# The second rows of the merge's operand in single steps, two latencies of the planned order, and the last block's sum ahead of its product

## The chip, the cores and the metric

The kernel runs on one core of a Trainium2 chip. A core has five engines that run their own instruction streams and wait for each other on semaphores: TensorE (PE, with weight loads as PEld) for matmuls, VectorE (DVE), ScalarE (ACT), GpSimd (POOL) and SyncE (SP), which issues nearly all DMAs, in the order of its stream. The metric is the device time of one execution in microseconds (us).

## The reference

One inference step of a one-layer encoder over 1024 prompt frames and 32 frames of a running stream, all in float32. After a norm and one wide input projection, two branches run side by side, gated linear attention (4 heads) and differential attention (8 heads); then they are merged:

```python
def out_merge(x, o_gla, o_diff, gg, dg, ma, mb, ...):
    yg = rmsnorm(o_gla, gla_norm_g).reshape(B, T, GLA_VAL) * silu(gg)
    yd = (rmsnorm(o_diff, diff_subln_g) * (1.0 - lambda_init)).reshape(B, T, DIFF_VAL) * silu(dg)
    merged = sigmoid(ma) * (yg @ w_proj_gla) + sigmoid(mb) * (yd @ w_proj_diff)
    return x + rmsnorm(merged @ w_out, post_norm_g)
```

Linear attention walks the frames in chunks: with the running sum `b` of the log decays, a chunk's keys are scaled by `exp(b_last - b)` and multiplied with the values into the new state, and each output is a part from the state and a part within the chunk.

## The kernel before

**Projections.** Everything is kept transposed: 128 channels on the partitions, T = 1056 frames (1024 + 32) along the free axis. A float32 operand is split in two, a rounded high part and the remaining low part, and a product is three matmuls (high by high, low by high, high by low). A projection of one block of 128 output channels runs over three chunks of 352 frames, with 8 blocks of the contraction, so 24 matmuls a chunk, into one PSUM bank; an `evac` then takes the bank away. Two banks serve these chunks in turn. Lines L517 to L519 are the matmuls of projections that run as `fill`, L493 to L495 those of the others. Weights come by DMA as `wr`, ScalarE rounds them to `wh` (L483) and GpSimd makes `wl` (L485).

**Stages and order.** Value projections run first, then, from about 216 us, linear attention; from about 543 us differential attention; from about 1137 us the merge's projections, and the output stage behind them. In the attention stages a planner (`Order`, `S.run`) writes TensorE's order: every thread of work yields steps with a cost, the events they need with a latency from the table `W`, and the PSUM banks they take; the planner takes the first thread in the list whose step is ready by its own clock, and projections (`fill`) come last in the list, so that they lie where the other threads wait. In linear attention these threads are a head's chain and the next head's preparation. The latencies are numbers in us; nothing in them changes what is computed. The other engines' instructions are placed by a scheduler that follows this order.

**Names in linear attention.** `k` is scaled by the decay on VectorE (L691), which marks the event `kd`; its transpositions through TensorE go to `ps_kt` (L699), ScalarE rounds them into `kdh` (L701) and VectorE makes `kdl` (L702). `po` is a chunk's output (L766 to L772), `o_sb` its copy in SBUF, scaled by the root mean square (L778); `ps_y` holds its transpositions (L785), `yt` (L788) their product with the gate, stored by DMA. `ps_kt` and `ps_y` take banks of the kind `t`; how long after its matmuls such a bank counts as taken is `kt_t` or `y_t`. `ar` (L619) is the masked part within a chunk; `t` in L573 to L578 is the next head's decay gate.

**The merge.** `w_proj_gla` has eight blocks, pg0 to pg7. Their evacuation, `tha = (1 + tha) * ps` (L1155), is on VectorE; behind a block's third chunk SP stores `tha` (to `ptd`) and loads a later `tha`. The second projection, `w_proj_diff` (L493 to L495), has the operand `yd`, eight rows of 128 channels called `Y` in the trace. Row k is made from the unscaled `ydr` in three steps: `split_yd(k)` multiplies it by `rsb` on VectorE (L1229), rounds it on ScalarE (L1230) into the high half, and subtracts on VectorE (L1231) for the low half; each `rsb` serves two rows and is 1 MB. These rows are made in the completion of pg3 to pg7: pg3 makes row 0, pg4 rows 1 and 2, pg5 row 3, pg6 rows 4 and 5, pg7 rows 6 and 7. In this part VectorE's order is as written. The second projection's evacuation begins with L1250 (`thb`), and the output weights `wout` are split into `cwh` (ScalarE) and `cwl` (VectorE, L1271) beside it.

**The end.** The output stage takes 128 frames at a time; for the last column block ScalarE squares `ps_c` and sums the row (L1300), VectorE multiplies by the weight of the norm (L1301), reduces the sums (L1308, L183), GpSimd takes the power (L184), and VectorE scales the row in two halves (L1317), which are stored. The halves of a block are done when the next block's sum is.

Of the kernel before, what the change touches and what calls it, by code (L numbers as in the profile page):

```python
# [11 lines left out]
F32 = mybir.dt.float32  # L12
# [3 lines left out]
ALU = mybir.AluOpType  # L16
# [9 lines left out]
KT = D // P  # L26
# [3 lines left out]
NQ = NP // P  # L30
# [9 lines left out]
BESIDE = range(3, KT)  # L40
# [14 lines left out]

W = {
# [3 lines left out]
    "tr_t": 2.27, "dv": 5.65, "at": 2.45, "pv_o": 1.6, "sdg": 1.84, "sdk": 21.35, "kc": 7.45, "ss_s": 3.69,  # L60
    "sp": 8.6, "st_t": 1.14, "sv": 3.44, "spt": 0.43, "so_o": 3.58, "so": 4.1, "so_t": 2.9, "yg0": 0.0,
    "yg": 1.18, "pg_b": 1.72, "p": 4.2, "p_w": 0.0042, "s_s0": 1.5, "s_w0": 0.0024, "s_s1": 0.3, "s_w1": 0.0012, "dg": 2.5,
# [68 lines left out]
def hybrid_step_kernel(ctx: ExitStack, tc: tile.TileContext, a):  # L131
# [3 lines left out]
    ve = nc.vector  # L135
    dma = nc.sync.dma_start
    st = nc.sync.dma_start

    def pool(name, bufs=1, **kw):
        return tc.alloc_tile_pool(name=name, bufs=bufs, **kw)  # L140
# [20 lines left out]
    def bank(name):  # L161
        return bank_of("pj", name)
# [18 lines left out]
    def rsqrt_mean(s, w, n, cnt):  # L181

        ve.tensor_scalar(s[0:w, 0:n], s[0:w, 0:n], 1.0 / cnt, EPS, op0=ALU.mult, op1=ALU.add)  # L183
        nc.gpsimd.tensor_tensor(s[0:w, 0:n], s[0:w, 0:n], mhalf[0:w, 0:n], op=ALU.pow)  # L184
# [91 lines left out]
    def sample_tiled(ps, x, w):  # L276

        for k in range(KT):
            r = k % 4 * NS
            mm(ps[r : r + NS], x[:, k, :], w[k], start=k < 4, stop=k >= 4, tile_position=(0, r))  # L280

    def sample_sum(dst, ps):
        act(dst, ps[32:64], AF.Copy)
        for r in (0, 64, 96):
            ve.tensor_tensor(dst, ps[r : r + NS], dst, op=ALU.add)
# [193 lines left out]
    def wtile(b):  # L479
        wr = wp.tile([P, KT, P], F32, tag="wr", bufs=1, name="wr")  # L480
        dma(wr, a["w128"][b])
        wh = odd(wp, KT, P, tag="wh", name="wh")
        act(wh, wr, AF.Copy)  # L483
        wl = odd(wp, KT, P, tag="wl", name="wl")
        nc.gpsimd.tensor_tensor(wl, wr, wh.bitcast(F32), op=ALU.subtract)  # L485
        return wh, wl
# [11 lines left out]
    def fill(jobs, src, then=None):  # L498

        w = wtile(jobs[0][0])  # L500
        for ji, (b, event, begin, needs) in enumerate(jobs):
            wh, wl = w
            evac = done = None
            for t0, n in CHUNKS:
                ps = None
                for k in range(KT):
                    if k % N["fill"] == 0:
                        yield 0.45 * N["fill"], (needs if ps is None else []), (["pj"] if ps is None else [])
                        if evac is None:
                            if ji + 1 < len(jobs):  # L510
                                w = wtile(jobs[ji + 1][0])
                            elif then is not None:
                                ahead.append(wtile(then))
                            evac, done = begin()
                        if ps is None:
                            ps = bank("ps_w")
                    mm(ps[:, :n], wh[:, k, :], src[k][:, 0, t0 : t0 + n], start=(k == 0), stop=False)  # L517
                    mm(ps[:, :n], wl[:, k, :], src[k][:, 0, t0 : t0 + n], start=False, stop=False)  # L518
                    mm(ps[:, :n], wh[:, k, :], src[k][:, 1, t0 : t0 + n], start=False, stop=(k == KT - 1))  # L519
                with tc.high_priority(offset=N["evac"]):  # L520
                    evac(ps[:, :n], slice(t0, t0 + n))
                S.free("pj", W["w_pj"])
            done()
            S.mark(event)

    ahead = []

    def silu_into(dst):

# [618 lines left out]
    def load_tha(j):  # L1148
        if j < KT:
            tha[j] = ld("tha")  # L1150
            dma(tha[j], thd[0, j])

    def pg_evac(j):
        def evac(ps, sl):
            ve.scalar_tensor_tensor(tha[j][:, sl], tha[j][:, sl], 1.0, ps, op0=ALU.add, op1=ALU.mult)  # L1155
        return evac
# [28 lines left out]
    def pg_job(j):  # L1185
        def begin():
            def done():
                st(ptd[j], tha[j])
                load_tha(j + 2)
                if j >= BESIDE[0]:  # L1190
                    for k in range(KT * (j - BESIDE[0]) // len(BESIDE), KT * (j + 1 - BESIDE[0]) // len(BESIDE)):
                        split_yd(k)
            return pg_evac(j), done
        return BLK_PG + j, ("pg", j), begin, []

# [6 lines left out]
    gpost = cp.tile([P, D], F32, name="gpost")  # L1202
    dma(gpost, a["gpost"].to_broadcast([P, D]))
    Y = x_pair("Y")
    yd = [Y[k // 6][:, k % 6] for k in range(KT)]
# [9 lines left out]
    rsb, ydr = {}, {}  # L1215

    def load_yd(k):
        if k < KT:
            ydr[k] = cp.tile([P, T], F32, tag=("cwr", "cwl")[k % 2], name="ydr")
            dma(ydr[k], ydd[k])  # L1220

    def load_rsb(k):
        if k < KT:
            rsb[k // 2] = cp.tile([P, 2, NP], F32, tag="cwh", name="rsb")
            dma(rsb[k // 2], rsd[k : k + 2, :].unsqueeze(0).to_broadcast([P, 2, NP]))

    def split_yd(k):
        r = ydr[k]
        ve.tensor_tensor(r[:, 0:NP], r[:, 0:NP], rsb[k // 2][:, k % 2], op=ALU.mult)  # L1229
        act(yd[k][:, 0, :], r, AF.Copy)  # L1230
        ve.tensor_tensor(yd[k][:, 1, :], r, yd[k][:, 0, :].bitcast(F32), op=ALU.subtract)  # L1231
        if k % 2:
            load_rsb(k + 1)
        load_yd(k + 2)

    load_rsb(0)
    load_yd(0)
# [4 lines left out]
    for j in range(KT):  # L1242
# [6 lines left out]
        def evac(ps, sl, th=th, pt=pt, y=y):  # L1249
            ve.scalar_tensor_tensor(th[:, sl], th[:, sl], 1.0, ps, op0=ALU.add, op1=ALU.mult)  # L1250
            ve.tensor_tensor(pt[:, sl], pt[:, sl], th[:, sl], op=ALU.add)
            act(y[:, 0, sl], pt[:, sl], AF.Copy, scale=0.5)
            ve.scalar_tensor_tensor(y[:, 1, sl], pt[:, sl], 0.5, y[:, 0, sl].bitcast(F32), op0=ALU.mult, op1=ALU.subtract)
# [20 lines left out]
    op = pool("op", reuse_waits="tile")  # L1274
    mgs = sample_whole(mg, op, "mgs")
    oga = xp.tile([P, 4, D], F32, tag="x2", name="oga")
    og = [oga[:, n] for n in range(4)]
# [6 lines left out]
    def out_block(u, n, i, wh, wl, raw):  # L1284
        csl = slice(u * 256, u * 256 + 256)
        w = P if i < NQ else NS
        t0 = i * P
        ps = (bank, dbank)[n % 2]("ps_c")[:, 0:256]
        if i < NQ:
            for k in range(KT):  # L1290
                mm(ps, mg[k][:, 0, t0 : t0 + P], wh[:, k, :], start=(k == 0), stop=False)  # L1291
                mm(ps, mg[k][:, 1, t0 : t0 + P], wh[:, k, :], start=False, stop=False)  # L1292
                mm(ps, mg[k][:, 0, t0 : t0 + P], wl[:, k, :], start=False, stop=(k == KT - 1))  # L1293
            src = ps
        else:
            sample_tiled(ps, mgs, raw)
            src = op.tile([NS, 256], F32, tag="tl", name="tl")
            sample_sum(src, ps)
        sqj = op.tile([P, 256], F32, tag="sqj", name="sqj")
        act(sqj[0:w], src[0:w], AF.Square, accum_out=ssq[0:w, i, u : u + 1])  # L1300
        ve.tensor_tensor(og[i][0:w, csl], src[0:w], gpost[0:w, csl], op=ALU.mult)  # L1301
        if u < 3:
            return

        if i == NQ - 1:
            ends.pop(0)()
        s1 = op.tile([P, 1], F32, tag="s1", bufs=2, name="s1")
        ve.tensor_reduce(s1[0:w], ssq[0:w, i, :], axis=AX.X, op=ALU.add)  # L1308
        rsqrt_mean(s1, w, 1, D)
        for e in ends:  # L1310
            e()
        ends.clear()

        def half(lo):
            def finish():
                h = slice(lo, lo + 512)
                ve.scalar_tensor_tensor(og[i][0:w, h], og[i][0:w, h], s1[0:w], xn[i][0:w, h], op0=ALU.mult, op1=ALU.add)  # L1317
                (nc.scalar.dma_start if i == NQ - 1 and lo else st)(a["y"][t0 : t0 + w, h], og[i][0:w, h])
                if lo and i in later[:2]:
                    load_rows(later[later.index(i) + 3])  # L1320
            return finish
        ends.extend([half(0), half(512)])
        if i == NQ - 1:
            for e in ends:
                e()
    for u in range(4):
# [5 lines left out]
        else:  # L1332

            raw = []
            for k in (0, 4):
                r = op.tile([P, D], F32, tag="xn", bufs=3, name="raw")
                r = r.rearrange("p (k n) -> p k n", k=4)
# [107 lines left out]
```

## Time and profile before

| | |
|---|---|
| median of three runs | 1445.84 us (1445.06 to 1446.31) |
| the profiled execution's own time | 1439.49 us |
| its span, first to last instruction | 1437.7 us |
| TensorE busy | 1394.2 us, 97% |
| VectorE, ScalarE, GpSimd busy | 717.0, 556.6, 299.9 us |
| mean granted clock of TensorE | 0.998 of full speed |

Times in the views below are from the span's start. A timeline row has the start, the duration, the engine, the line, the operation with its output and input, and in brackets how long the engine had been idle before it and what released it. Durations of pipelined matmuls overlap, so the pace is read from their starts.

### The profile page before, as it was taken

What the parts mean: (1) busy time and instruction counts of PE and PEld (TensorE: products, weight loads), DVE (VectorE), ACT (ScalarE), POOL (GpSimd) and SP (SyncE); (2) the same over time, 40 slices, a digit from 0 to 9 for tenths busy, and PEclk for the clock granted to TensorE, in tenths of its full rate; (3) what the DMA queues carried; (4) which work ended last, traced back from release to release, by engine and by line L of the source; (5) the groups of instructions that cost most, each with busy time, mean ns of one, the idle gap of its engine ahead of it and who ended that gap; (6) DMA issues with size and microseconds to landing.
All of it is one profiled execution on the core that took longest, in us unless ns stands there. A gap on an engine that the chain in (4) does not pass through costs nothing.

```text
span 1437.7 us, 22643 instructions
## 1 busy us (share of the span) xinstructions
PE 1394.2 (97%) x9074; PEld 1288.8 (90%) x9074; DVE 717.0 (50%) x1448; ACT 556.6 (39%) x1164; POOL 299.9 (21%) x194
## 2 busy tenths in 40 slices
PE   8999999999999999999999999999999999999997
PEld 7687789889989899998989898989999899899997
DVE  5522005666555342565655555565565424555425
ACT  4523104535344232454444444454554422221321
POOL 1200002222223223222232222222221122122002
PEclk9999999999999999999999999999999999999999
DMA  8422111122222233112221322122232475643434
GB/s 308 163 103 98 46 44 57 44 75 85 84 71 76 74 122 100 61 64 87 72 78 52 92 66 86 54 93 66 78 94 76 146 263 203 242 166 128 161 114 150
DMA packets 65251, 152.42 MB, mean 106 GB/s; under 512 B 9664, under 2 KB 28512, under 8 KB 63728
## 3 DMA queue, kind: packets, MB, share of 16 engines
q1 hardware_dynamic: 64992, 150.60, 31.5%
q8 instruction: 75, 1.23, 0.4%
q14 instruction: 40, 0.33, 0.1%
q10 hardware_dynamic: 144, 0.26, 0.0%
HBM read 108.60 MB, written 40.08 MB: 103 GB/s over the span
## 4 chain that ended last, share of the span: by engine, by line
PE 58%; DVE 5%; ACT 1%; issue 1%; DMA 0%; POOLq 0%; DVEq 0%; ACTq 0%
PE ps_w L517 11%; PE ps_w L518 11%; PE ps_w L519 11%; PE ps_s L944 4%; PE ps_t L1006 2%; PE ps_c L1291 2%; PE ps_c L1293 2%; PE ps_c L1292 2%; PE ps_w L495 2%; PE ps_w L493 2%; PE ps_w L494 2%; PE po L1020 1%; PE po L1021 1%; DVE nm L948 1%; PE po L1019 1%
## 5 line engine op out<-in xcount | busy, mean ns | idle before, releaser
L517 PE MATMUL ps_w<-X,wh 128*128 128x352 f32 x1344 | 449.9, 335 | 0.7 <-ACT vo L308 0.4
L518 PE MATMUL ps_w<-X,wl 128*128 128x352 f32 x1344 | 435.2, 324 | 0.8 <-issue 0.8
L519 PE MATMUL ps_w<-X,wh 128*128 128x352 f32 x1344 | 433.5, 323 | 0.0
L485 POOL TENSOR_TENSOR wl<-wr,wh 128x1024 fp32r<-128x1024 f32 x72 | 177.7, 2469 | 561.8 <-ACT wh L483 497.5
L517 PEld LDWEIGHTS ps_w<-X,wh 128*128 128x128 f32 x1344 | 252.8, 188 | 8.4 <-issue 4.7
L518 PEld LDWEIGHTS ps_w<-X,wl 128*128 128x128 f32 x1344 | 253.2, 188 | 1.1 <-issue 1.1
L519 PEld LDWEIGHTS ps_w<-X,wh 128*128 128x128 f32 x1344 | 252.5, 188 | 0.0
L950 ACT ACTIVATE p<-ps_s,nm 128x256 f32<-128x256 f32 (+7 forms) x128 | 94.5, 740 | 63.0 <-DVE nm L948 60.7
L483 ACT ACTIVATE wh<-wr 128x1024 fp32r<-128x1024 f32 x72 | 76.1, 1056 | 68.0 <-PE ps_w L519 40.8
L328 PE MATMUL ps_v<-wh,X 128*128 128x512 f32 x248 | 98.7, 398 | 0.0
L329 PE MATMUL ps_v<-wh,X 128*128 128x512 f32 x248 | 97.6, 394 | 0.8 <-DVE X L245 0.8
L330 PE MATMUL ps_v<-wl,X 128*128 128x512 f32 x248 | 98.3, 396 | 0.0
L948 DVE TENSOR_REDUCE nm<-ps_s 128x1 f32<-128x256 f32 (+7 forms) x128 | 93.2, 753 | 0.0
L1009 DVE TENSOR_TENSOR al<-ps_t,ah 128x512 fp32r<-128x512 f32 (+2 forms) x96 | 53.2, 554 | 35.6 <-ACT ah L1008 34.3
L1008 ACT ACTIVATE ah<-ps_t 128x512 fp32r<-128x512 f32 (+2 forms) x96 | 47.0, 489 | 60.8 <-PE ps_t L1006 60.3
L495 PE MATMUL ps_w<-Y,wh 128*128 128x352 f32 x192 | 61.9, 324 | 0.8 <-DVE Y L1231 0.7
L493 PE MATMUL ps_w<-Y,wh 128*128 128x352 f32 x192 | 62.0, 324 | 0.5 <-DVE thb L1250 0.5
L494 PE MATMUL ps_w<-Y,wl 128*128 128x352 f32 x192 | 61.8, 324 | 0.0
L308 ACT ACTIVATE vo<-ps_v 128x512 f32<-128x512 f32 x32 | 19.0, 595 | 105.7 <-PE ps_v L330 105.3
L1024 DVE SCALAR_TENSOR_TENSOR osb<-po,gs_half,sg 128x256 f32<-128x256 f32 x32 | 15.5, 483 | 88.3 <-ACT sqo L1023 88.3
L328 PEld LDWEIGHTS ps_v<-wh,X 128*128 128x128 f32 x248 | 46.7, 188 | 12.7 <-issue 1.7
L329 PEld LDWEIGHTS ps_v<-wh,X 128*128 128x128 f32 x248 | 46.7, 188 | 12.5 <-DVE X L245 1.7
(319 smaller groups left out, 2681.1 us busy)
## 6 DMA issues: line engine op xcount, KB each, us to landing
wr<-w SPq DMA_DIRECT2D x72, 512.0 KB
thd<-gate SPq DMA_DIRECT2D x16, 528.0 KB
wr<-wv SPq DMA_DIRECT2D x16, 512.0 KB
xn<-xn SPq DMA_DIRECT2D x12, 512.0 KB
newk<-pair SPq DMA_DIRECT2D x8, 528.0 KB
y<-ygd SPq DMA_DIRECT2D x8, 528.0 KB
tha<-thd SPq DMA_DIRECT2D x8, 528.0 KB
ydr<-ydd SPq DMA_DIRECT2D x8, 528.0 KB
```

The costliest lines, as they stand in the source:

```text
L328: mm(ps, xk[:, 0, t0 : t0 + P], wh[:, k, :], start=(k == 0), stop=False)
L329: mm(ps, xk[:, 1, t0 : t0 + P], wh[:, k, :], start=False, stop=False)
L330: mm(ps, xk[:, 0, t0 : t0 + P], wl[:, k, :], start=False, stop=(k == KT - 1))
L485: nc.gpsimd.tensor_tensor(wl, wr, wh.bitcast(F32), op=ALU.subtract)
L493: mm(ps[:, :n], wh[:, k, :], src[k][:, 0, t0 : t0 + n], start=(k == 0), stop=False)
L494: mm(ps[:, :n], wl[:, k, :], src[k][:, 0, t0 : t0 + n], start=False, stop=False)
L495: mm(ps[:, :n], wh[:, k, :], src[k][:, 1, t0 : t0 + n], start=False, stop=(k == KT - 1))
L517: mm(ps[:, :n], wh[:, k, :], src[k][:, 0, t0 : t0 + n], start=(k == 0), stop=False)
L518: mm(ps[:, :n], wl[:, k, :], src[k][:, 0, t0 : t0 + n], start=False, stop=False)
L519: mm(ps[:, :n], wh[:, k, :], src[k][:, 1, t0 : t0 + n], start=False, stop=(k == KT - 1))
L948: ve.tensor_reduce(nm, ps[:, 0:w], axis=AX.X, op=ALU.max, negate=True)
L950: act(p[:, 0:w], ps[:, 0:w], AF.Exp, bias=nm, accum_out=sums[m])
```

## The change

Three parts. First, in the merge, `split_yd` is cut in two: `scale_yd(k)` (multiplication, the rounding copy, and behind an odd row the load of the next `rsb`) and `split_yd(k)` (subtraction and the load of a later row). They are called one at a time in the order scale 0, split 0, scale 1, ... behind the evacuation of each of the fifteen chunks of pg3 to pg7; the last but one takes two steps. Second, in the planner's table the latency from `kd` to the transpositions goes from 3.96 to 5.8, and the time for which `ps_y`'s bank stays taken from 0.64 to 1.65. Third, the last block of the output stage reduces its sum and starts the power before it multiplies by the norm's weight.

```diff
 W = {
-    "a_t": 1.14, "as_t": 0.79, "kd": 3.96, "kt_t": 0.3, ...
+    "a_t": 1.14, "as_t": 0.79, "kd": 5.8, "kt_t": 0.3, ...
-    "po_o": 0.67, "sg": 0.65, "on": 6.76, "y_t": 0.64, ...
+    "po_o": 0.67, "sg": 0.65, "on": 6.76, "y_t": 1.65, ...
...
                     evac(ps[:, :n], slice(t0, t0 + n))
                 S.free("pj", W["w_pj"])
+                if event in beside:
+                    beside[event]()
...
                 load_tha(j + 2)
-                if j >= BESIDE[0]:
-                    for k in range(KT * (j - BESIDE[0]) // len(BESIDE), KT * (j + 1 - BESIDE[0]) // len(BESIDE)):
-                        split_yd(k)
...
-    def split_yd(k):
+    def scale_yd(k):
         r = ydr[k]
         ve.tensor_tensor(r[:, 0:NP], r[:, 0:NP], rsb[k // 2][:, k % 2], op=ALU.mult)
         act(yd[k][:, 0, :], r, AF.Copy)
-        ve.tensor_tensor(yd[k][:, 1, :], r, yd[k][:, 0, :].bitcast(F32), op=ALU.subtract)
         if k % 2:
             load_rsb(k + 1)
+
+    def split_yd(k):
+        ve.tensor_tensor(yd[k][:, 1, :], ydr[k], yd[k][:, 0, :].bitcast(F32), op=ALU.subtract)
         load_yd(k + 2)
+    steps = [f for k in range(KT - 1) for f in ((scale_yd, k), (split_yd, k))]
+    steps = [[f] for f in steps[:-1]] + [[steps[-1], (scale_yd, KT - 1)], [(split_yd, KT - 1)]]
+
+    def beside_chunk():
+        for f, k in steps.pop(0):
+            f(k)
+    beside.update({("pg", j): beside_chunk for j in BESIDE})
...
-        ve.tensor_tensor(og[i][0:w, csl], src[0:w], gpost[0:w, csl], op=ALU.mult)
+        def product():
+            ve.tensor_tensor(og[i][0:w, csl], src[0:w], gpost[0:w, csl], op=ALU.mult)
         if u < 3:
+            product()
             return
-        if i == NQ - 1:
+        last = i == NQ - 1
+        if last:
             ends.pop(0)()
+        else:
+            product()
...
         rsqrt_mean(s1, w, 1, D)
+        if last:
+            product()
```

Lines of the changed file from L520 on are two higher, and more behind the merge: the evacuation is L1157, the multiplication L1228, the subtraction L1234, `thb` L1261, `cwl` L1282; the product of the last stage L1313, the sum L1325, the halves L1336.

On VectorE at the end of pg3 to pg7, before, one block's burst (of pg4; `Y_12709` holds rows 0 to 5, `Y_12710` rows 6 and 7):

```order
L1155 SCALAR_TENSOR_TENSOR tha<-tha,ps_w 128x352 x3
L1229 TENSOR_TENSOR ydr<-ydr,rsb 128x1024
L1231 TENSOR_TENSOR Y_12709<-ydr,Y_12709 128x1056
L1229 TENSOR_TENSOR ydr<-ydr,rsb 128x1024
L1231 TENSOR_TENSOR Y_12709<-ydr,Y_12709 128x1056
```

and now, from pg7's second chunk on into the second projection:

```order
L1157 SCALAR_TENSOR_TENSOR tha<-tha,ps_w 128x352
L1234 TENSOR_TENSOR Y_12710<-ydr,Y_12710 128x1056
L1228 TENSOR_TENSOR ydr<-ydr,rsb 128x1024
L1157 SCALAR_TENSOR_TENSOR tha<-tha,ps_w 128x352
L1234 TENSOR_TENSOR Y_12710<-ydr,Y_12710 128x1056
L1282 TENSOR_TENSOR cwl<-cwr,cwh 128x512
L1261 SCALAR_TENSOR_TENSOR thb<-thb,ps_w 128x352
```

An evacuation now stands between any two chunks' steps, only this chunk has two, and the first `cwl` comes ahead of the second projection's first evacuation.

ScalarE in linear attention, around the third head's transpositions of `k`, before:

```order
L701 ACTIVATE kdh<-ps_kt 32x128
L531 ACTIVATE sg<-ps_w 128x352
L701 ACTIVATE kdh<-ps_kt 128x512
L573 ACTIVATE t_4225<-ps_z,vecs 128x352
L577 ACTIVATE t_4225<-t_4225 128x1056
L701 ACTIVATE kdh<-ps_kt 128x512
```

and now:

```order
L703 ACTIVATE kdh<-ps_kt 32x128
L575 ACTIVATE t_4225<-ps_z,vecs 128x352
L579 ACTIVATE t_4225<-t_4225 128x1056
L703 ACTIVATE kdh<-ps_kt 128x512
L580 ACT_TABLE_LOAD
L580 ACTIVATE t_4225<-t_4225 128x1056
L703 ACTIVATE kdh<-ps_kt 128x512
```

Both large copies from the bank `t` moved behind an activation of the gate. On TensorE 12 more of the projection's matmuls now stand ahead of the first `ps_kt` transposition of a head (42, before 30) and 6 more between the two groups of four `ps_y` transpositions (12, before 6), while in the last head only 12 instead of 36 stand between its eighth block's `po` and the eight `ps_y`. On VectorE in the third head both `yt` now come ahead of the state's update.

VectorE at the very end, before:

```order
L1301 TENSOR_TENSOR ogwwl_14038<-ps_c,gpost 128x256
L1317 SCALAR_TENSOR_TENSOR ogwwh_14037<-ogwwh_14037,s_15057,xn 128x512
L1308 TENSOR_REDUCE s_15095<-ssq 128x1
L183 TENSOR_SCALAR s_15095<-s_15095 128x1
L1317 SCALAR_TENSOR_TENSOR ogwwh_14037<-ogwwh_14037,s_15057,xn 128x512
L1317 SCALAR_TENSOR_TENSOR ogwwl_14038<-ogwwl_14038,s_15095,xn 128x512 x2
```

and now:

```order
L1336 SCALAR_TENSOR_TENSOR ogwwh_14037<-ogwwh_14037,s_15057,xn 128x512
L1325 TENSOR_REDUCE s_15094<-ssq 128x1
L183 TENSOR_SCALAR s_15094<-s_15094 128x1
L1313 TENSOR_TENSOR ogwwl_14038<-ps_c,gpost 128x256
L1336 SCALAR_TENSOR_TENSOR ogwwh_14037<-ogwwh_14037,s_15057,xn 128x512
L1336 SCALAR_TENSOR_TENSOR ogwwl_14038<-ogwwl_14038,s_15094,xn 128x512 x2
```

The sum moved ahead of the last block's product, behind the first half of the block before.

More of the change, by code (lines that the diff above doesn't have):

```diff
@@ L522, in fill @@
                 S.free("pj", W["w_pj"])
+                if event in beside:
+                    beside[event]()
             done()
             S.mark(event)
-    ahead = []
+    ahead, beside = [], {}
     def silu_into(dst):
```

4 rows, old and new, of the table W are left out of this document.

## The prediction, made before the changed kernel was run

> **What bounds the kernel now.** I read the page's head and busy times first, then busy time by stage.
>
> ```profile
> span 1437.7 us, 22643 instructions
> PE 1394.2 (97%) x9074; PEld 1288.8 (90%) x9074; DVE 717.0 (50%) x1448; ACT 556.6 (39%) x1164; POOL 299.9 (21%) x194
> ```
>
> ```profile
> 216.00:543.00 327.00, 312.45 (x2038) 300.15 (x2037) 180.88 (x303) 141.95 (x283) 86.98 (x53) 1.00 0.24 76
> 1137.00:1243.00 106.00, 99.16 (x614) 97.56 (x615) 36.97 (x43) 23.95 (x27) 20.26 (x8) 0.98 0.68 240
> ```
>
> TensorE is the bound: 97% busy, and the change leaves its matmuls as they are. An edit gains only what TensorE stood still, or ran slowly. The second view's columns are the window, its length, busy time of PE, PEld, DVE, ACT, POOL, then granted clock, DMA share and GB/s: the linear attention (216 to 543) has 14.5 us without a matmul, the merge's first projection (to 1243) 6.8. Which waits these are, the view of PE's waits says (sum, times, longest):
>
> ```profile
> PE ps_w L517 <- DVE tha L1155: 4.6, 2, 3.0
> PE ps_y L785 <- DVE yt L788: 3.5, 4, 0.9
> PE ps_kt L699 <- DVE k L691: 3.2, 2, 1.7
> PE ps_as L625 <- DVE ar L619: 1.5, 1, 1.5
> PE pf L587 <- DVE yt L788: 0.7, 1, 0.7
> ```
>
> The first is the merge's, the others the linear attention's. For the merge, PE's timeline (start, duration, idle before and its releaser):
>
> ```profile
> 1207.71 0.33 PE L518 MATMUL ps_w<-y,wl 128*128 128x352 f32 x1
> ...
> 1209.32 0.32 PE L519 MATMUL ps_w<-y,wh 128*128 128x352 f32 x1
> 1212.67 0.66 PE L517 MATMUL ps_w<-y,wh 128*128 128x352 f32 x1 [3.04 <-DVE tha L1155]
> ...
> 1215.48 0.41 PE L517 MATMUL ps_w<-y,wh 128*128 128x352 f32 x1
> 1215.73 0.32 PE L518 MATMUL ps_w<-y,wl 128*128 128x352 f32 x1
> ...
> 1237.13 0.32 PE L519 MATMUL ps_w<-y,wh 128*128 128x352 f32 x1
> 1238.96 0.43 PE L517 MATMUL ps_w<-y,wh 128*128 128x352 f32 x1 [1.51 <-DVE tha L1155]
> 1239.23 0.32 PE L518 MATMUL ps_w<-y,wl 128*128 128x352 f32 x1
> ...
> 1242.92 0.33 PE L493 MATMUL ps_w<-Y,wh 128*128 128x352 f32 x1
> ...
> 1252.83 0.43 PE L493 MATMUL ps_w<-Y,wh 128*128 128x352 f32 x1 [0.45 <-DVE thb L1250]
> ```
>
> From 1207.71 to 1209.32 are ten matmuls: 0.161 us each, so a chunk of 24 takes 3.86. What holds the matmul of 1212.67 is VectorE's timeline:
>
> ```profile
> 1202.41 1.22 DVE L1229 TENSOR_TENSOR ydr<-ydr,rsb 128x1024 f32<-128x1024 f32 x1
> 1204.78 2.23 DVE L1231 TENSOR_TENSOR Y<-ydr,Y 128x1056 fp32r<-128x1056 f32 x1 [1.16 <-ACT Y L1230]
> 1208.56 1.23 DVE L1229 TENSOR_TENSOR ydr<-ydr,rsb 128x1024 f32<-128x1024 f32 x1 [1.55 <-DMA rsb<-rsd]
> 1210.93 1.26 DVE L1231 TENSOR_TENSOR Y<-ydr,Y 128x1056 fp32r<-128x1056 f32 x1 [1.15 <-ACT Y L1230]
> 1212.11 0.95 DVE L1155 SCALAR_TENSOR_TENSOR tha<-tha,ps_w 128x352 f32<-128x352 f32 x2
> ```
>
> Two rows of the second product come in one burst: multiply, wait for ScalarE's copy, subtract, wait for a load, again. VectorE is tied from 1202.41 to 1212.11; two chunks' evacuations (L1155) queue behind it, and with two banks the third chunk finds none. The chain of waits names the load:
>
> ```profile
> 1203.65 4.88 DMA rsb<-rsd
> ```
>
> **The change part by part.** *Merge.* Lost now: 1212.67 - 1209.32 - 0.16 = 3.19, and behind it slow matmuls: 1212.67 to 1215.73 are ten steps in 3.06 where 1.61 is normal, 1.45 more. The second burst costs 1239.23 - 1237.13 - 0.32 = 1.78. The third (row seven) makes the next projection start poorly: its first two chunks take 1252.83 - 1242.92 = 9.91 against 7.72, 2.19. Together 8.6. The clock in the window around the first is quoted here:
>
> ```profile
> 1202.00:1218.50 16.50, 13.46 (x76) 13.17 (x75) 7.52 (x8) 3.51 (x4) 2.73 (x1) 0.90 0.65 226
> ```
>
> By the Trainium skill, "TensorE: Matmul & The Clock Gate", Part 1, about 3.4 us of idleness puts the matmul clock to half rate until activity releases it; here a gap of 3.04 already did, and one of 1.51 did not. By the page's figure the 3.04 gap would have cost no slow steps and the merge would gain 7.2, not 8.6; the row decides.
>
> After the change one step stands behind each chunk's evacuation: multiply (1.22) or subtract (1.26 to 2.33), beside 0.52 for the evacuation itself: at most 2.85 of every 3.86 us, and only pg7's second chunk has two steps (2.3 + 1.2 + 0.5 = 4.0), taken up by the second bank. The copy (1.09 on ScalarE) has a whole chunk between. No operation is added. The load of rsb, needed 4.9 us after its issue, is now issued behind the odd row's multiply, and its user comes two chunks less that multiply later, 7.7 - 1.2 = 6.5. So the whole 8.6 goes. What can take some back: the next projection's first evacuation now stands behind a first cwl subtraction on VectorE, which needs the 1 MB load of wout. That projection's first chunk will run from 1242.92 - 4.64 - 1.78 = 1236.5 to 1240.4. The load takes the buffer of row six, free when the subtraction in pg7's second chunk ends: that chunk is evacuated at 1236.5 - 3.9 = 1232.6, and 0.5 + 2.3 later is 1235.4. With rsb's 4.9 for as many bytes it lands at 1240.3, and a late evacuation holds TensorE only from the third chunk on, at 1244.2. Bounds: 8.6 if none is late, 7.0 if this stall is back at half its old size. I take 8.6.
>
> *Linear attention.* No instruction is added; the planner, told that `kd` takes 5.8 and that the bank `t` stays taken 1.65, moves projection matmuls. Removed: both waits for k (12 more matmuls, 1.93 us, now precede the first transposition; longest wait 1.7), two of the four for yt (0.9 each; six more matmuls), and L619's and pf's, whose producers now come first: 3.2 + 1.8 + 1.5 + 0.7 = 7.2, and 0.16 for each restart (1.67 lost at 1238.96 where 1.51 is printed), 8.2.
>
> Cover is paid for elsewhere, since the projections' work is fixed. In the last head 36 matmuls stood between the last `po` and the eight ps_y transpositions; now 12:
>
> ```profile
> 519.37 0.28 PE L772 MATMUL po<-sl,qh 128*128 128x256 f32 x1
> ```
>
> ```profile
> 522.48 1.23 DVE L778 TENSOR_TENSOR o_sb<-o_sb,ss 128x1024 f32<-128x1024 f32 x1 [1.19 <-POOL ss L184]
> ...
> 455.94 0.75 DVE L788 SCALAR_TENSOR_TENSOR yt<-ps_y,gg_half,sg 128x512 f32<-128x512 f32 x1 [1.58 <-DMA ygd<-yt]
> ```
>
> o_sb is ready at 522.48 + 1.23 = 523.71; TensorE would be there at 519.49 + 12 x 0.161 = 521.42: a new stall of 2.3. In the first head 18 matmuls and three small ones remain: 1.1. In heads 0 to 2 ScalarE does the gate's exponential ahead of the kdh copy on which the next transpositions' bank hangs:
>
> ```profile
> 415.67 1.28 ACT L578 ACT_TABLE_LOAD   x1
> ```
>
> ```profile
> L577 ACT ACTIVATE t<-t 128x1056 f32<-128x1056 f32 x4 | 4.3, 1086 | 0.1
> ```
>
> Each exponential is 1.09; a third of it is hidden, I take 0.75, three times 2.25 (bounds 0 and 3 x 2.4, where the table load of 1.28 and a second exponential's start are ahead too). In head 2 both yt now precede the state's update on VectorE, and the second waits for the first one's store as at 455.94: 1.5 (bounds 0 and 2.5). New: 2.3 + 1.1 + 2.25 + 1.5 = 7.2. Net gain 1.0, with -5 (all removed, half of the new hidden) to +3 (the upper bounds) around it.
>
> *Tail.* The end hangs on VectorE and one POOL power:
>
> ```profile
> 1428.43 1.42 DVE L1317 SCALAR_TENSOR_TENSOR ogwwh<-ogwwh,s,xn 128x512 f32<-128x512 f32 x2
> 1428.65 0.94 POOL L184 TENSOR_TENSOR s<-s,mhalf 128x1 f32<-128x1 f32 x1 [1.78 <-DVE s L183]
> ...
> 1430.33 0.19 ACT L1300 ACTIVATION_READ_ACCUMULATOR sqj<-ps_c 128x1 f32 x1
> 1430.55 0.42 DVE L1301 TENSOR_TENSOR ogwwl<-ps_c,gpost 128x256 f32<-128x256 f32 x1 [0.70 <-ACT sqj L1300]
> 1430.89 0.74 DVE L1317 SCALAR_TENSOR_TENSOR ogwwh<-ogwwh,s,xn 128x512 f32<-128x512 f32 x1
> 1431.55 0.15 DVE L1308 TENSOR_REDUCE s<-ssq 128x1 f32<-128x4 f32 x1
> ...
> 1432.99 1.41 DVE L1317 SCALAR_TENSOR_TENSOR ogwwl<-ogwwl,s,xn 128x512 f32<-128x512 f32 x2 [0.44 <-POOL s L184]
> ```
>
> The sum was ready at 1430.52 and L1308 began at 1431.55. Now the preceding block's half can run while ScalarE squares, from 1429.8, when VectorE is through with the block before (its factor is ready at 1429.6), and the reduction follows the accumulator at 1430.6; the product then hides under POOL's 0.92. Gain 0.9; 0.34 if the half still starts late.
>
> **Sum.** -8.6 - 1.0 - 0.9 = -10.5 on the profiled execution of 1439.49 (1.8 around its span). The shown runs' median, 1445.84, lies 6.35 above that, a difference that I take as the same for both kernels: 1435.3.
>
> **The rivals.** *The linear attention loses.* The planner moves cover, and its upper bounds hold: +3, then -6.5 in all, 1439.3. For it speaks that no matmul is saved; against, that both long waits for k lie where 1.93 more are laid. A gap of more than 3 us at the last head would add 1.45 of slow steps to that. *It gains fully*: -5, 1431.3; for it the four kinds of waits named above, against it the 2.3 at 519. *The merge gives part back at the next projection's start* through wout: 1.6 to 4, 1437 to 1439. *Slower.* SP issues in order. rsb's load for rows four and five now stands behind pg4's store and a `tha` load; before, such a load went out about as long after the store as here:
>
> ```profile
> 1202.52 0.32 SPq L1188 DMA_DIRECT2D ptd<-tha  x1
> ...
> 1207.45 0.38 SPq L1151 DMA_DIRECT2D tha<-thd  x1
> ```
>
> If each of the three loads slips behind the next block's store, three chunks or 11.6 us, it lands 4.9 + 11.6 = 16.5 us after the multiply. Allowed are 12.0: the multiply ends 1.7 after its chunk's evacuation begins, and the one that needs the load must be done, with the next evacuation (1.7 together), when the bank is wanted four chunks (15.4) after the first; each then costs 4.5 of stall and 1.45 of slow steps, 17.9 for three: -10.5 + 17.9 = +7.4, 1453.2. It decides from 12.0 - 4.9 = 7.1 us of delay in SP. Against it: from store to load were 4.9 above. *The change does nothing here*: then -1.9 remains, 1444; the program's order has single steps, so this is nearly out.
>
> By the Trainium skill, "DMA: Bandwidth & Descriptors", a wait on a semaphore is made by the issuing sequencer before dispatch; that is this rival's mechanism, and no run here shows it.
>
> **How the numbers follow.** Likeliest 0.47, own range 1433 to 1437.5; linear attention loses 0.18; gains fully 0.12; merge returns part 0.12; slower 0.06; nothing, 0.05. The range 1430.5 to 1442 leaves out slower, nothing and a little of each. Runs tell 0.2% (2.9 us) from no change: faster than 1442.9 holds for the first four but for the far ends, 0.84; same 0.09; slower 0.07.
>
> **What shows it.** In the new trace VectorE has L1157 and then one of L1228 or L1234 through pg3 to pg7; no wait of PE on `tha` over 0.5 us; granted clock 1.00 from 1183 to 1236; the stage ends 6 to 9 us sooner in its own length. PE's waits have no k row over 0.5, and a ps_y row near 2.3 in the last head. The last reduction starts within 0.2 us of the accumulator. I am wrong if PE waits on `tha` or Y again, or if the linear attention's length leaves 322 to 330 us.

## The result, and the profile after

The changed kernel takes 1434.73 us (median of seven, 1432.75 to 1439.52) against 1445.84 us before (median of seven, 1441.33 to 1448.39). The ratio is 0.994, 95% interval 0.9923 to 0.9957: 8.7 us faster, with 6.2 to 11.1 in the interval; the two medians lie 11.1 apart, at the far end of it. The profiled execution took 1432.75 us. The page's head and busy times:

```profile
span 1431.0 us, 22651 instructions
PE 1392.9 (97%) x9074; PEld 1289.3 (90%) x9074; DVE 713.1 (50%) x1448; ACT 556.0 (39%) x1164; POOL 300.4 (21%) x194
```

Cutting both timelines of TensorE at the first matmul of each stage shows where the 6.7 us between the two spans lie (us; the experiments' profiled executions are added for later use). Below, "linear attention" is the second row, "pg" the fourth (the merge's first projection) and "second projection" the fifth:

| stretch, up to the first ... | before | changed | e1 | e2 | e3 |
|---|---|---|---|---|---|
| projection beside linear attention (`ps_w`) | 216.8 | 218.8 | 217.6 | 217.9 | 217.6 |
| score of differential attention (`ps_s`) | 368.0 | 369.06 | 368.0 | 371.9 | 363.2 |
| matmul of pg0 | 557.4 | 557.3 | 557.55 | 557.4 | 558.6 |
| matmul of the second projection | 100.8 | 94.3 | 94.3 | 102.9 | 94.75 |
| matmul of the output stage | 94.9 | 92.8 | 92.6 | 94.95 | 92.6 |
| last matmul | 91.8 | 91.8 | 91.8 | 91.8 | 91.8 |
| end | 8.1 | 6.9 | 6.9 | 8.1 | 6.9 |

The first stretch, 2.1 longer, contains nothing that was changed; 216.8 to 220.0 occur among all the executions. Without it the span fell by 8.8: merge -8.56 (-6.47 and -2.09), end -1.20, linear attention +1.03.

**The merge went as foreseen.** VectorE's timeline in pg5 to pg7 of the changed kernel, an excerpt:

```profile
1212.67 0.52 DVE L1157 SCALAR_TENSOR_TENSOR tha<-tha,ps_w 128x352 f32<-128x352 f32 x1 [2.21 <-PE ps_w L519]
1213.11 1.25 DVE L1234 TENSOR_TENSOR Y<-ydr,Y 128x1056 fp32r<-128x1056 f32 x1
1216.52 0.52 DVE L1157 SCALAR_TENSOR_TENSOR tha<-tha,ps_w 128x352 f32<-128x352 f32 x1 [2.16 <-PE ps_w L519]
1217.66 1.23 DVE L1228 TENSOR_TENSOR ydr<-ydr,rsb 128x1024 f32<-128x1024 f32 x1 [0.62 <-DMA rsb<-rsd]
```

One step stands behind each evacuation, VectorE waits for TensorE again instead of the other way round, and the load of `rsb` is late by 0.62 without harm to TensorE. SP sends that load off 0.03 us behind the odd row's multiplication (the one of 1209.24, which ends at 1210.45):

```profile
1210.48 0.32 SPq L1224 DMA_DIRECT2D rsb<-rsd  x1
```

Busy time by window, for 1199 to 1236 (columns as in the prediction):

```profile
1199.00:1236.00 37.00, 37.00 (x232) 37.00 (x232) 15.60 (x19) 8.62 (x8) 8.60 (x3) 1.00 0.80 276
```

TensorE has no gap in 37 us, at full clock.

**The end** (timeline of all engines, an excerpt):

```profile
1424.81 0.20 ACT L1311 ACTIVATION_READ_ACCUMULATOR sqj<-ps_c 128x1 f32 x1
1425.03 0.16 DVE L1325 TENSOR_REDUCE s<-ssq 128x1 f32<-128x4 f32 x1
...
1425.30 0.41 DVE L1313 TENSOR_TENSOR ogwwl<-ps_c,gpost 128x256 f32<-128x256 f32 x1
```

The reduction starts at 1425.03, as soon as the accumulator is read (1424.81 + 0.20); before it started 1.03 behind that.

**Linear attention is the surprise.** PE's waits in the changed kernel:

```profile
PE ps_y L787 <- DVE yt L790: 5.6, 3, 4.3
PE ps_kt L701 <- DVE kdl L704: 3.4, 4, 1.3
...
PE ps_y L787 <- DVE o_sb L780: 2.2, 1, 2.2
```

The waits for `k` and `ar` are gone and `o_sb` costs 2.2 in the last head, where 2.3 was worked out. But one wait for `yt` is 4.3, longer than any before. It is in the first head; PE's timeline there:

```profile
321.87 0.60 PE L787 MATMUL ps_y<-ident,o_sb 128*128 128x128 f32 x4
326.73 1.11 PE L787 MATMUL ps_y<-ident,o_sb 128*128 128x128 f32 x4 [4.26 <-DVE yt L790]
...
328.23 0.49 PE L517 MATMUL ps_w<-X,wh 128*128 128x352 f32 x1
328.52 0.49 PE L518 MATMUL ps_w<-X,wl 128*128 128x352 f32 x1
```

Slow matmuls follow (steps of 0.29 where 0.16 is normal): the granted clock is 0.50 from 324.07 to 330.90, and TensorE was busy for 4.17 us of that:

```profile
324.07:330.90 6.83, 4.17 (x16) 4.17 (x17) 5.61 (x7) 2.08 (x3) 1.90 (x1) 0.50 0.45 152
```

So half of 4.17, some 2.1 us, were lost by the slow clock. VectorE and GpSimd in the same time:

```profile
322.56 3.45 DVE L684 TENSOR_TENSOR al<-ar,ah 128x1024 fp32r<-128x1024 f32 x2
325.94 0.73 DVE L790 SCALAR_TENSOR_TENSOR yt<-ps_y,gg_half,sg 128x512 f32<-128x512 f32 x1
```

```profile
323.56 2.41 POOL L485 TENSOR_TENSOR wl<-wr,wh 128x1024 fp32r<-128x1024 f32 x1 [3.41 <-ACT wh L483]
```

`yt` is queued behind the two subtractions for `al` (128x1024 and 32x32), which take 3.45 together. Before, the same pair in the same place took

```profile
320.62 1.31 DVE L682 TENSOR_TENSOR al<-ar,ah 128x1024 fp32r<-128x1024 f32 x2
```

1.31, and GpSimd's wl began only at 326.32. The second of the two, which takes 0.17 otherwise, now ends when wl ends (323.56 + 2.41 = 325.97).

### The profile page after: what moved, and what is told of

Read it like the earlier page. It is cut to its first block, busy times and chain, and to the rows that moved or that the text cites. A ratio compares the mean times of both kernels' runs of the same rounds, so it can differ in the third digit from the quotient of the medians.

```text
span 1431.0 us, 22651 instructions
## 1 busy us (share of the span) xinstructions
PE 1392.9 (97%) x9074; PEld 1289.3 (90%) x9074; DVE 713.1 (50%) x1448; ACT 556.0 (39%) x1164; POOL 300.4 (21%) x194
## 4 chain that ended last, share of the span: by engine, by line
PE 60%; DVE 4%; ACT 1%; issue 0%; DVEq 0%; POOL 0%; ACTq 0%; POOLq 0%
PE ps_w L517 12%; PE ps_w L518 11%; PE ps_w L519 11%; PE ps_s L946 4%; PE ps_t L1008 2%; PE ps_w L493 2%; PE ps_w L494 2%; PE ps_w L495 2%; PE ps_c L1302 2%; PE ps_c L1304 2%; PE ps_c L1303 2%; PE po L1022 1%; PE po L1023 1%; DVE nm L950 1%; PE po L1021 1%; PE ps_w L1174 1%
```

## The experiments

Two theories at the outset. **A**: the merge and the end bring all the gain; the two latencies together cost about 1 us, because they take cover away at the `ps_y` of the first and the last head. **B**: the latencies help too, and the one profiled execution hides it.

### e1: without the latencies

```diff
-    "a_t": 1.14, "as_t": 0.79, "kd": 5.8, ...
+    "a_t": 1.14, "as_t": 0.79, "kd": 3.96, ...
-    "po_o": 0.67, "sg": 0.65, "on": 6.76, "y_t": 1.65, ...
+    "po_o": 0.67, "sg": 0.65, "on": 6.76, "y_t": 0.64, ...
```

> The merge's single steps and the earlier sum, with both latencies of the table as before (3.96 and 0.64). Theory A (the new order of the linear attention costs about 1 us): from the first ps_w to the first ps_s the linear attention takes 368.0 us as before, not 369.05; pg 94.3 and the second projection 92.8 as in the changed kernel; the tail 6.9; no wait of 4.3 us of ps_y. About 9.8 us less than before in all, 1 us less than the changed kernel: 1434 to 1436, ratio 0.993. Theory B (the new latencies help, and the profiled execution hid it): the linear attention is slower than 369.05 and the kernel at least 1 us slower than the changed one.

Measured: 1432.46 us, ratio 0.9918 (0.9899 to 0.9938). Linear attention 368.0, pg 94.3, second projection 92.6, end 6.9, all as theory A has them, and the time is 1.5 us below the 1434 to 1436 expected; in median e1 is 2.3 us faster than the changed kernel, though the two intervals overlap. The merge and the end alone save 11.8 us by the ratio, more than the 9.9 that their stretches show.

### e2: the latencies alone

```diff
 # the kernel before
-    "a_t": 1.14, "as_t": 0.79, "kd": 3.96, ...
+    "a_t": 1.14, "as_t": 0.79, "kd": 5.8, ...
-    "po_o": 0.67, "sg": 0.65, "on": 6.76, "y_t": 0.64, ...
+    "po_o": 0.67, "sg": 0.65, "on": 6.76, "y_t": 1.65, ...
```

> Only the two latencies of the table changed, merge and last block as before. Theory A: the linear attention 369.0 us (before 368.0), with the 4.3 us wait of ps_y in the first head and the 2.2 us one in the last; merge 100.8 and 94.9 as before; ratio 1.0007, no difference that the runs can tell. Theory B: linear attention below 368 and ratio below 0.999.

Measured: 1445.61 us, ratio 1.0001 (0.9981 to 1.0022). No gain, as A has it; the waits of 4.46 and 2.19 are there. Linear attention is 371.9, though, and pg 102.9, 2 to 3 us longer than foreseen with the same waits. Windows of this execution around the last head's wait and around the merge's second burst:

```profile
525.00:540.00 15.00, 11.74 (x65) 10.68 (x64) 8.25 (x17) 5.01 (x16) 5.17 (x3) 0.77 0.39 132
1244.00:1251.00 7.00, 6.47 (x31) 6.47 (x32) 1.67 (x5) 0.72 (x1) 0.00 (x0) 0.76 0.77 290
```

(behind a gap that PE's timeline of e2 shows as

```profile
1244.53 0.43 PE L517 MATMUL ps_w<-y,wh 128*128 128x352 f32 x1 [1.93 <-DVE tha L1155]
```

for the second), and of the changed kernel and of the kernel before at the same places:

```profile
525.00:540.00 15.00, 11.68 (x79) 10.53 (x78) 8.81 (x18) 5.14 (x16) 7.04 (x5) 1.00 0.50 161
```

```profile
1237.00:1244.00 7.00, 5.49 (x34) 5.20 (x33) 3.01 (x5) 1.01 (x2) 0.00 (x0) 1.00 0.99 368
```

The granted clock is 0.77 where it is 1.00 in the others: 15 x 0.23 = 3.5 and 7 x 0.24 = 1.7 us, less where TensorE stood idle meanwhile. So what a gap costs differs between executions, and one profile need not show it.

### e3 and e4: one latency at a time

```diff
 # the changed kernel; e3
-    ... "on": 6.76, "y_t": 1.65, ...
+    ... "on": 6.76, "y_t": 0.64, ...
 # e4
-    ... "kd": 5.8, ...
+    ... "kd": 3.96, ...
```

> As the changed kernel, but with y_t as before (0.64): only the latency of kd is new. The last head then has 30 matmuls between its last po and the eight ps_y (12 in the changed kernel), the first head 30 instead of 18. Theory A' (cover is lost where the two numbers act together): both waits for k (3.2) gone, two waits for yt of 0.9 stay, no 2.2 us wait in the last head, the first head's ps_y wait 1 to 2 us instead of 4.3 and no slow matmuls behind it: linear attention 365 to 366. Rival (any new order costs as much as it hides): 368 to 369.

> As the changed kernel, but with kd as before (3.96): only the bank time of ps_y is new. Theory A': the two waits for yt of 0.9 and the 1.5 for ar go, the waits for k (1.5 and 1.75) stay, the last head keeps 36 matmuls ahead of its eight ps_y and has no 2.2 us wait, the first head's ps_y wait is 1 to 2 us: linear attention 365.5 to 366.5. Rival: 368 to 369.

Measured for e3: 1427.84 us, ratio 0.988 (0.9859 to 0.9901), better than the changed kernel beyond both intervals, and 4.6 us better than e1. Linear attention is 363.2, shorter than expected. PE's waits of e3:

```profile
PE ps_y L787 <- DVE yt L790: 6.1, 6, 1.6
```

Six small waits for `yt`, none over 1.6, none for `k`, none for `o_sb`. In the first head the `al` pair takes 1.31 there, and wl begins at 324.01, behind `yt`.

Measured for e4: 1430.72 us, ratio 0.9898 (0.9879 to 0.9916), 1.7 better than e1, with overlapping intervals. Linear attention is 368.95 in its profile, not 365.5 to 366.5: a wait for `sl` of 1.99 at 292 had not been expected, with slow matmuls behind it. Some 1.1 of it is the pattern of the first head again, VectorE and GpSimd at that place:

```profile
290.81 1.51 DVE L763 TENSOR_TENSOR sl<-s_new,sh 128x256 fp32r<-128x256 f32 x1
...
292.45 0.40 DVE L763 TENSOR_TENSOR sl<-s_new,sh 128x256 fp32r<-128x256 f32 x1
```

```profile
290.78 1.26 POOL L718 TENSOR_TENSOR vl<-vr,vh 128x512 fp32r<-128x512 f32 x1 [1.73 <-ACT vh L717]
```

The same subtraction takes 0.40 alone and 1.51 beside `vl`. That the number for `kd` is worth several us alone (4.6 against e1), and nothing in the medians together with `y_t`, is what neither theory had said.

### e5: one whole row behind every second chunk

```diff
-    steps = [[f] for f in steps[:-1]] + [[steps[-1], (scale_yd, KT - 1)], [(split_yd, KT - 1)]]
+    steps = [s for k in range(KT) for s in ([(scale_yd, k), (split_yd, k)], [])][:-1]
```

> As the changed kernel, but one whole row (multiply, copy, subtract) behind every second chunk and nothing behind the others: VectorE again waits for ScalarE's copy, but never makes two rows in one go. Theory A (the stalls came from two rows between two evacuations, not from VectorE's wait for the copy): a row takes 0.5 + 1.2 + 1.2 + 2.25 = 5.2 us of the 7.7 of two chunks, the second bank takes up the 1.3 by which the next evacuation is late, so pg stays at 94.3 with no wait on tha; only the second projection starts later by 1 to 2 us (92.64 becomes 94 to 94.5), since row 7 is now made whole behind the last chunk. Theory B (the wait for the copy itself is what stalls): waits of 1 to 1.5 us on tha come back and pg is 97 or more.

Measured: 1435.6 us, ratio 0.9955 (0.9937 to 0.9972); pg 94.9 with no wait on `tha` in pg3 to pg7, second projection 93.7 (+1.05). PE in the second projection:

```profile
1245.33 0.43 PE L495 MATMUL ps_w<-Y,wh 128*128 128x352 f32 x1 [0.79 <-DVE Y L1234]
```

Theory A holds, with the second projection 0.3 short of the 94 expected. Two of the eight subtractions took 2.25 and 2.24 us here, as long as in the bursts of before, and VectorE waited 1.1 us for one load of `rsb`, still without a wait of TensorE on `tha`. So two rows between two evacuations were the fault, not VectorE's wait for the copy; what single steps gain over this is the last row's readiness, 1 us.

### e6: the load of rsb a chunk later

```diff
-        if k % 2:
-            load_rsb(k + 1)

     def split_yd(k):
         ve.tensor_tensor(yd[k][:, 1, :], ydr[k], yd[k][:, 0, :].bitcast(F32), op=ALU.subtract)
+        if k % 2:
+            load_rsb(k + 1)
         load_yd(k + 2)
```

> As the changed kernel, but the load of rsb goes out behind the odd row's subtraction instead of its multiplication, one chunk later. Theory A (there is slack of several us in this load): VectorE waits about 3 us for rsb ahead of rows 2, 4 and 6, the evacuation behind it is about 1 us late, and TensorE does not wait: pg 94.3, second projection 92.6. Rival (the load is near the edge, with SP's waits ahead of it): waits of PE on tha of 1 to 3 us, three times, pg 97 to 103.

Measured: 1435.39 us, ratio 0.9951 (0.9935 to 0.9966); pg 94.45, second projection 92.6, no wait on `tha` in pg3 to pg7. But on the chip the edit did not move the load: the longest wait for it is 0.45 instead of 3, because SP still sends it off 0.03 us behind the multiplication, ahead of the subtraction (VectorE and SP, an excerpt):

```profile
1209.41 1.77 DVE L1228 TENSOR_TENSOR ydr<-ydr,rsb 128x1024 f32<-128x1024 f32 x1
1211.21 0.32 SPq L1224 DMA_DIRECT2D rsb<-rsd  x1
...
1213.28 1.25 DVE L1232 TENSOR_TENSOR Y<-ydr,Y 128x1056 fp32r<-128x1056 f32 x1
...
1217.67 1.23 DVE L1228 TENSOR_TENSOR ydr<-ydr,rsb 128x1024 f32<-128x1024 f32 x1 [0.45 <-DMA rsb<-rsd]
```

So e6 is the changed kernel over again, and how late this load may go out stays open. What speaks against the prediction's slower case is only that SP did not delay it, here or in the changed kernel.

The linear attention of e6 is the changed kernel's too, and in this execution the first head went another way: wl begins behind `yt`.

```profile
322.42 0.73 DVE L790 SCALAR_TENSOR_TENSOR yt<-ps_y,gg_half,sg 128x512 f32<-128x512 f32 x1
323.08 1.97 DVE L691 TENSOR_TENSOR b<-b 128x32 f32<-128x32 f32 x1
```

```profile
322.65 2.35 POOL L485 TENSOR_TENSOR wl<-wr,wh 128x1024 fp32r<-128x1024 f32 x1 [3.87 <-ACT wh L483]
```

The longest wait for `yt` is 1.40 instead of 4.26. Even so the stretch takes 368.97, because the clock was at half twice, in the first and in the last head:

```profile
321.17:328.00 6.83, 5.43 (x22) 5.03 (x21) 5.62 (x8) 3.37 (x5) 2.35 (x1) 0.50 0.56 194
525.97:532.80 6.83, 5.98 (x28) 5.58 (x28) 3.10 (x6) 1.00 (x4) 2.01 (x1) 0.50 0.47 164
```

TensorE was busy for 5.43 + 5.98 us there and lost half of that, 5.7 us. Taken off (an estimate), the linear attention is 363.3 in e6, and by the same account 367.0 in the changed kernel's profile: the same program with and without GpSimd's wl ahead of `yt`.

### e7 and e8: al on GpSimd

```diff
 # e7 the changed kernel, e8 that of e3
-            ve.tensor_tensor(al[0:r, c, 0:w], ar[0:r, c, 0:w], ah[0:r, c, 0:w].bitcast(F32), op=ALU.subtract)
+            nc.gpsimd.tensor_tensor(al[0:r, c, 0:w], ar[0:r, c, 0:w], ah[0:r, c, 0:w].bitcast(F32), op=ALU.subtract)
```

> The changed kernel, with the subtraction that makes al (128x1024, four heads) on GpSimd instead of VectorE; in the first head VectorE then has yt two short instructions behind the b subtraction. Theory A (the 4.3 us wait of ps_y is yt queued behind al, with the projection's matmuls gone that covered it): this wait falls to about 1 us, the slow matmuls behind it are gone, linear attention 364.5 instead of 369.05, the kernel 4 to 5 us faster than the changed one. Rival (yt waits for something else, or GpSimd's subtractions slow VectorE as much): wait still 3 us or more, or linear attention above 367.5.

> The kernel with only the latency of kd new (e3), and al on GpSimd. Theory A: there the first head's wait was 1.6 us and yt still has k's multiplication ahead of it, so little is left: wait about 1 to 1.5, linear attention 362.5 to 363.2, within 1 us of e3's time. Rival: GpSimd delays the projection's weights or VectorE, linear attention 364 or more.

Measured: e7 1432.27 us, ratio 0.9927 (0.9914 to 0.9939), linear attention 368.2; the wait in the first head is 2.83, not 1. e8 1432.95 us, ratio 0.9926 (0.9909 to 0.9942), 5 us worse than e3, with linear attention 368.9 and a wait of 5.19 instead of 1 to 1.5: the rival there too. VectorE and GpSimd of e7 in the first head:

```profile
321.41 2.34 DVE L691 TENSOR_TENSOR b<-b 128x32 f32<-128x32 f32 x1
323.68 0.73 DVE L790 SCALAR_TENSOR_TENSOR yt<-ps_y,gg_half,sg 128x512 f32<-128x512 f32 x1
```

```profile
320.22 3.70 POOL L684 TENSOR_TENSOR al<-ar,ah 128x1024 fp32r<-128x1024 f32 x2 [1.22 <-ACT ah L683]
```

With `al` gone from VectorE, the next short instruction in front of `yt`, a subtraction of 128x32, takes 2.34 (0.17 before) beside GpSimd's `al`. So the queue was named rightly and its size wrongly: the delay follows GpSimd's subtractions, whichever instruction of VectorE meets them. That is the rival that I had written down for e7. In e8 the same subtraction takes 2.34, and `yt` stands behind `k`'s multiplication, which needs its result. With the 2.7 us lost by slow clock taken off (half of 5.41 busy at 0.50) e8's linear attention is 366.2, and e3's, without slow clock, 363.2: as between the changed kernel and e6, the meeting ahead of `yt` goes with 3 to 4 us.

### e9: kd 5.3

```diff
 # the changed kernel
-    "a_t": 1.14, "as_t": 0.79, "kd": 5.8, ...
+    "a_t": 1.14, "as_t": 0.79, "kd": 5.3, ...
```

> As the changed kernel, but kd 5.3 instead of 5.8 (y_t 1.65 as changed): the planner then lays 36 matmuls ahead of each head's first ps_kt (42 in the changed kernel, 30 before) and 24 ahead of the last head's eight ps_y (12 and 36), and 24 in the first head. Theory A (the loss lies in the two places where cover was taken away, the gain in the waits for k and yt): waits for k of 0.5 to 0.8 in two heads, none for yt of 0.9, none of 2.2 us in the last head, the first head's ps_y wait 2 to 2.6; linear attention 364 to 366 without slow clock, time 1429 to 1432, between e3 and the changed kernel. Rival (what counts is whether GpSimd's wl falls on VectorE in the first head, not the cover): a wait of ps_y of 4 us or more there and linear attention 367 to 369.

Measured: 1434.0 us, ratio 0.9931 (0.9912 to 0.995), linear attention 370.0: the rival, and a us beyond its 369. Cover is better in all the places named (the last head's `o_sb` costs 0.97, the waits for `k` 0.51 at most), and yet

```profile
325.93 1.11 PE L787 MATMUL ps_y<-ident,o_sb 128*128 128x128 f32 x4 [4.51 <-DVE yt L790]
```

```profile
322.89 2.32 DVE L691 TENSOR_TENSOR b<-b 128x32 f32<-128x32 f32 x1
```

```profile
322.51 2.66 POOL L485 TENSOR_TENSOR wl<-wr,wh 128x1024 fp32r<-128x1024 f32 x1 [3.27 <-ACT wh L483]
```

wl begins at 322.51, and the 128x32 subtraction, with `yt` behind it, meets it: 2.32.

### e10: the small parts first

```diff
 # the changed kernel; the same for b's two subtractions
-        for r, c in ((P, slice(0, 8)), (NS, slice(8, 9))):
+        for r, c in ((NS, slice(8, 9)), (P, slice(0, 8))):
```

> The changed kernel, with the 32-column parts of b and al emitted ahead of the 1024-column parts (TensorE's order unchanged), so that in the first head no tiny subtraction stands between al and yt on VectorE when GpSimd's wl begins. Theory (the 4.3 us wait of ps_y is mostly a 0.2 us subtraction that cannot run beside wl and stands for 2.3 us with yt behind it): al's large part is nearly done when wl begins, yt runs at about 324.1 to 324.5 instead of 325.9 and the wait of ps_y falls to 2.2 to 2.8. Rival (any VectorE instruction of two SBUF inputs that meets wl stands until wl ends): al's large part now meets it and takes 3 us or more, the wait stays at 4 or above.

Measured: 1433.61 us, ratio 0.9933 (0.992 to 0.9947), linear attention 368.7, the wait 2.03. It is no clean test: in this execution wl came at 326.30, behind `yt`, so nothing met it. As an observation it fits: the same TensorE order without the meeting waits 2.03 instead of 4.26. The 2.03 is still above the 1.1 of the prediction, and half clock followed it all the same.

## Why the prediction was right, and where it was not

The time, 1435.3 foreseen and 1434.73 measured, is right by more than it deserves. The profiled execution became 6.7 us shorter, not 10.5, and the step from it to the median was 2.0 us, not 6.35: two errors of 3.8 and 4.4 that cancel by luck. Of the 3.8, 2.1 lie in the first stretch, where nothing was changed, and 2.0 in the linear attention.

- **Merge, -8.6.** Measured in the stretches -8.56 (e1: -8.7). The mechanism held: one step behind each evacuation, no wait of TensorE on `tha`, the clock at 1.00, no wait at the first `cwl` (the second projection takes 92.6 to 92.8; its 24 chunks of 3.86 are 92.7). Only `rsb` was tighter than worked out: VectorE waited 0.62 and 0.66 us for two of its loads, where 4.9 of an allowed 6.5 us had been put down, and TensorE did not feel it. By e5 the stall came from two rows in one go. That the term fits so well is luck: the profile of before was an execution in which the second burst's gap of 1.51 went by without slow matmuls. In e2 the same burst left 1.93 and the clock fell. That may be why e1 gains 11.8 by the ratio and 9.9 in the stretches; it is an inference, since only profiled executions can be looked into.
- **"A difference that I take as the same for both kernels", 6.35.** This step failed. The changed kernel's median lies 2.0 above its profiled execution, not 6.35. The median granted clock is 0.993 in both kernels (seven executions of the changed one, and the seventeen of the one before that ran beside e1 to e4), while the profiled ones had 0.998 and 0.996: the profiled execution of before was an unusually undisturbed one, and 0.005 of 1440 is 7 us. The first stretch's 2.1 us, by chance, lay on the other side.
- **Linear attention, -1.0.** Measured +1.03 in the stretch, and +2.3 in the medians of e1 and the changed kernel. The waits that should go went (`k`, `ar`, two of `yt`), and the new ones at the last head (2.19 for 2.3), for `kdl` (3.4 against 1.5, foreseen +2.25) and for `yt` in the later heads came out. The step that failed is "in the first head 18 matmuls and three small ones remain: 1.1". It counted when `o_sb` is ready; `o_sb` was in time, and the wait is the second group's, for the bank that `yt` empties. What VectorE had queued ahead of `yt`, and that GpSimd's wl would now fall on it, was not looked at. The wait was 4.26 with wl on it, 1.40 and 2.03 without (e6, e10). The slow clock of the first and last heads (2.1 us lost in this profile, 5.7 in e6's) is no term of the sum either; without it the stretch would be 367.0, 1.1 shorter than before, so that the net of -1.0 would be met, but by other terms than the forecast's. The rival "the linear attention loses" is what happened, at +1 instead of its +3; its upper bounds, added up, give 2.3 + 1.1 + 7.2 + 2.5 - 8.2 = +4.9, not +3.
- **End, -0.9.** Measured -1.20 in the changed kernel, -0.9 to -1.2 over all the executions with this part.
- **The slower case, loads of rsb behind SP's waits.** It did not occur: SP sent the loads off 0.03 us behind the multiplication, where a delay of 7.1 would have decided it. What such a delay costs was not tested, since e6 made none.
- **What shows it.** A ps_y row of 2.3 in the last head was foreseen, and linear attention between 322 and 330 us in length: to the last group of `ps_y` it was 328.0 (before 325.9), within.

The best version found is e3, the changed kernel without the new bank time: 1427.84 us.

## What to carry to other kernels

A measured latency that is put right in a planner's table is not a gain in itself: it moves filler work, and the place that pays is the one whose cover went. Work out for each wait that loses filler what the other engines have queued ahead of its producer, and which engine's work the moved filler drags with it (here the weights' split on GpSimd). Before a profiled execution's stalls are summed, compare its granted clock with that of the other executions: gaps of 2 us and more carry a further cost that a single profile may show or not.

## What the runs showed of the hardware

**A VectorE instruction with two SBUF operands stands while GpSimd works on its own.** In the first head, the 128x32 subtraction of `b` takes 0.17 when GpSimd is idle (before, e1, e3, e4) and 1.97 to 2.34 when it falls on wl or al (e6, e7, e8, e9); the 0.40 of `sl` became 1.51 in e4. Such an instruction that comes while GpSimd works runs only when that ends: 325.97 for the tiny `al`, and in the merge before, where wl was

```profile
1203.16 2.73 POOL L485 TENSOR_TENSOR wl<-wr,wh 128x1024 fp32r<-128x1024 f32 x1 [8.83 <-ACT wh L483]
```

and ended at 1205.89, the subtraction of 1204.78 ended at 1207.01, its own 1.25 less 0.13 later. One that had begun before GpSimd, like the large `al`, was not held up noticeably. Counted over the twelve profiles, of VectorE's TENSOR_TENSOR instructions that began while a large TENSOR_TENSOR of GpSimd had 0.3 us or more to go, 208 of 213 with both operands in SBUF ended at GpSimd's end plus their usual duration less 0.11 to 0.15 us; the other five, not held, began within the first 0.3 us of GpSimd's instruction. The 193 with one operand in PSUM were not held at all, and neither were the 12 with both operands in SBUF that met a MEMSET of GpSimd. With single steps the merge's eight subtractions no longer meet wl; the groups by line have a mean of

```profile
L1234 DVE TENSOR_TENSOR Y<-ydr,Y 128x1056 fp32r<-128x1056 f32 x8 | 10.2, 1276 | 0.0
```

1276 ns, where L1231 had 1888. The Trainium skill, "GPSIMD Engine Reference", says in its table of the engine's properties that the SBUF interfaces are shared with VectorE and that instructions with two SBUF inputs contend; the runs agree, and show that the contention is not a slowing in proportion: a tenth of a microsecond can become two.

**A gap of 2 to 2.3 us sometimes halves the clock behind it, and where it lies decides.** The twelve profiled executions have the same gap of 2.27 to 2.28 at the start of the merge or just ahead of it; in five of them (e3, e4, e5, e6, e8) the clock over the eight us around is 0.79, in seven 1.00. The gap of 2.19 in the last head was followed by clocks of 0.62 to 0.81 in four of six executions (e2, e5, e6, e10), by 1.00 in two (the changed kernel and e7). Between 216 and 1300 us, all eight gaps of 2.8 and more (3.04 before, 4.26 in the changed kernel, 3.01 and 4.46 in e2, 4.19, 2.83, 5.19 and 4.51 in e5, e7, e8 and e9) were followed by slow matmuls, and so were 1.93 in e2, 1.99 in e4 and 2.03 in e10; of those below 1.9 that stand alone, none.

The traces show why. Within a trace the stretches at half clock begin on a grid: in e2 those of 324.06, 528.86, 1218.35 and 1245.65 begin 0, 60, 262 and 270 steps of 3.413 us after the first. Cut along this grid from 216 to 1300 us, the twelve profiles have 21 steps in which TensorE had 1.93 us or more without a matmul, and half clock followed all 21; it followed two of the six with 1.86 to 1.91, and, at full clock, only one of all the others (1.64 in e6). So the gap of 2.19 costs where one step holds it, as in e10 (busy 1.26 of 3.41, then clock 0.50), and not where the grid cuts it, as in the changed kernel (busy 1.67 and 2.13):

```profile
524.50:527.92 3.41, 1.26 (x8) 0.96 (x7) 2.21 (x3) 1.41 (x2) 2.60 (x3) 1.00 0.41 115
527.92:531.33 3.41, 2.53 (x11) 2.13 (x12) 0.75 (x1) 0.00 (x0) 2.23 (x1) 0.50 0.49 190
```

```profile
525.46:528.87 3.41, 1.67 (x11) 1.37 (x9) 1.85 (x3) 1.76 (x4) 2.53 (x3) 1.00 0.29 70
528.87:532.28 3.41, 2.13 (x17) 1.89 (x18) 1.55 (x3) 0.00 (x0) 2.65 (x1) 1.00 0.60 237
```

The Trainium skill, "TensorE: Matmul & The Clock Gate", Part 1, puts the idle window at about 3.4 us and calls it free-running. The grid agrees with that, but here idle time well under 3.4 us, about 1.9 within a window, already met it.
